# A decoder layer's mixer: the attention halves of the output projection in tiles of their own, the mLSTM output in pairs of heads

## The chip, the cores and the metric

The kernel runs on one core of one Trainium2 chip. The metric is the device time of one execution in microseconds (us). TensorE is the engine for matrix products, VectorE, ScalarE and GpSimd work elementwise, and SyncE issues the transfers from memory.

## The reference, cut to what matters

One layer on 256 tokens of width 1024: a half-step SwiGLU FFN, a mixer, a second half-step FFN, and a last norm. Each of the three parts has its RMS norm, and shift, scale and gate that come from a vector `c` by a matrix `w_ada`. The mixer runs attention (8 heads of 64) beside an mLSTM (4 heads of 128):

```
o_a = rmsnorm(attention(q_a, k_a, v_a), attn_norm)
h_m = (h_m - mu) * rsqrt(var + EPS) * mlstm_norm
o_m = (h_m + mlstm_skip * x_conv) * silu(z)
return concat([o_a, o_m]) @ w_out
```

## The kernel before, in words

All activations lie transposed, 128 features by 256 tokens in a tile; a group of 1024 features is eight tiles. Every big product is made of three products: weight and activation are each split into a rounded high part and a remainder (`whi`, `wlo`; `hh`, `hl`), and `mm3` adds high times high, remainder times high and high times remainder. ScalarE copies the high part, VectorE subtracts for the remainder (`hilo` for activations, `split_piece` for weights, in pieces of 1024 columns).

Weights come in chunks of 1 MB. `weights()` hands out the next chunk; it first asks for the load of the chunk three further on and the split of the next one. There are four buffers of raw chunks and five each of `whi` and `wlo`. The 72 columns of `w_ada` are loads too, 512 KB each into three `ada` buffers, and each is followed by one VectorE product with a sum (`junk`). `side(0)` issues the next such job. All loads go through SyncE's queue in the order in which the program issues them.

The order on the other engines is made by a scheduler, except where `act.on`, `dve.on` or `pe.on` is set: those instructions keep the program's order among themselves. The `junk` products of the mixer keep it too.

The mixer's end, in program order: `tiles(...)` makes the gate `z` in two groups of two heads, each from one chunk, reading all of `hh` and `hl`. Between them stand the last attention heads (`weigh`), the sums of the mLSTM heads (`m_sums`), and `a_out`, which makes the attention's norm, scales the four tiles `oa[j]` in place and splits `oa[0]` into `mix0h` and `mix0l`. After the second gate group come `m_factors` (the mLSTM's norm factors in `rows`, four rows of 256), the split of `oa[1..3]` into `hh[:,1..3]`, the Silu of the gate, and `m_out_pre`. The output projection follows: four chunks of `w_out` of two steps each, k = 0 to 7, each step 24 products. `m_spread` broadcasts `rows` over the partitions into two banks of tag `b`, and `m_out(h)` finishes one head and splits it into `hh[:,4+h]`.

The softmax weights of a pair of attention heads lie in a tile `pr` of 128 x 768 numbers, in two buffers by turns; `turn(j)` transposes them.

Of the kernel before, what the change touches and what calls it, by code (L numbers as in the profile page):

```python
# [11 lines left out]
F32R = mybir.dt.float32r  # L12
BF16 = mybir.dt.bfloat16
AF = mybir.ActivationFunctionType
ALU = mybir.AluOpType
AX = mybir.AxisListType

P = 128
T = 256
# [5 lines left out]
NH = 4  # L25
# [11 lines left out]
C_MN = 124  # L37
C_SK = 128
# [23 lines left out]
def layer(ctx: ExitStack, tc: tile.TileContext, i, out: bass.AP):  # L62
    nc = tc.nc
    act, dve, pool, pe = (Ordered(tc, e) for e in (nc.scalar, nc.vector, nc.gpsimd, nc.tensor))
# [29 lines left out]
    def const(shape, dt, name):  # L94
        return cst.tile(shape, dt, tag=name, name=name)
# [10 lines left out]
    sm = const([P, NSM], F32, "sm")  # L106
# [114 lines left out]
    def weights(ahead=3):  # L221

        n = used[0]
        used[0] += 1
        load_to(n + ahead)
        split_to(n + 1)
        return parts[n]
# [6 lines left out]
    def mm3(ps, w, b0, xh, xl, start, stop):  # L234
        hi, lo = part(w, b0, P)
        pe.matmul(ps, hi, xh, start=start, stop=False, skip_group_check=True)
        pe.matmul(ps, lo, xh, start=False, stop=False, skip_group_check=True)
        pe.matmul(ps, hi, xl, start=False, stop=stop, skip_group_check=True)
# [77 lines left out]
    hh = const([P, ND, WS], F32R, "hh")[:, :, 0:W]  # L316
    hl = const([P, ND, WS], F32R, "hl")[:, :, 0:W]
# [249 lines left out]
    def side(*on):  # L567

        for o in on:
            if jobs:  # L570
                jobs.pop(0)(o)
# [8 lines left out]
    pinned[0] = True  # L580
    for c in range(2):
        w = weights()
        side(*[0] * (2 - c))
        for d4 in range(4):
            d = c * 4 + d4
            for h in range(NH):
                mm3(px[h][:, 0:W], w, d4 * 512 + h * P, hh[:, d], hl[:, d], start=(d == 0), stop=(d == 7))
            if d == 0:
                r = rstd_of([acc, nxt_sq[0]], pre=False)
# [17 lines left out]
def mixer(tc, nc, i, mp, L):  # L607
    act, dve, pool, pe, sp = L["act"], L["dve"], L["pool"], L["pe"], L["sp"]
    nm, bank, t256, as32, dma = L["nm"], L["bank"], L["t256"], L["as32"], L["dma"]
    weights, part, mm3, hilo = L["weights"], L["part"], L["mm3"], L["hilo"]  # L610
    sm, hh, hl, tmp, eps_t = L["sm"], L["hh"], L["hl"], L["tmp"], L["eps_t"]
# [3 lines left out]
    side, jobs = L["side"], L["jobs"]  # L615

    def mt(shape, name, dt=F32, tag=None, bufs=1):
        return mp.tile(shape, dt, name=nm(name), tag=tag or name, bufs=bufs)
# [62 lines left out]
    xc = mt([P, NH, T], "xc")  # L681
# [42 lines left out]
    st = {}  # L724
# [60 lines left out]
    cn = mt([P, NH, T], "cn")  # L785
# [7 lines left out]
    def m_sums(h):  # L793
        if h == 0:
            st["prow"] = bank("a")
        prow = st["prow"]
        pn = bank("b" if h == 3 else "m")
        pe.matmul(pn[:, 0:T], vm[:, 0, h], wE[h][:, 0:T], start=True, stop=False, skip_group_check=True)
        pe.matmul(pn[:, P:T], vm[:, 1, h], wE[h][:, T:384], start=False, stop=True, skip_group_check=True)
        pe.matmul(prow[0:4, 0:T], ohc[:, h], wE[h][:, 0:T], start=(h == 0), stop=False, skip_group_check=True)  # L800
        pe.matmul(prow[0:4, P:T], ohc[:, h], wE[h][:, T:384], start=False, stop=(h == NH - 1),
                  skip_group_check=True)
        act.activation(cn[:, h], pn[:, 0:T], AF.Copy)
        s = st["sq", h] = t256("sq", bufs=3)
        act.activation(s, cn[:, h], AF.Square)

    def m_vars(h):
        pe.matmul(st["prow"][0:4, T:2 * T], ohc[:, h], st["sq", h], start=False, stop=(h == NH - 1),
                  skip_group_check=True)
# [15 lines left out]
        spread(rs)  # L825


    mix0 = [mt([P, T], name, F32R) for name in ("mix0h", "mix0l")]

    def mix(k):  # L830
        return mix0 if k == 0 else (hh[:, k, 0:T], hl[:, k, 0:T])

    zs = mt([P, NH, T], "zs")

    def z_silu(h2):
        z2 = zs[:, 2 * h2:2 * h2 + 2]
        tc.keep_in_program_order(act.activation(z2, z2, AF.Silu))

    def m_out_pre(h):

        dve.scalar_tensor_tensor(cn[:, h], cn[:, h], sm[:, C_MN + h:C_MN + h + 1], zs[:, h], ALU.mult, ALU.mult)
        dve.scalar_tensor_tensor(xc[:, h], xc[:, h], sm[:, C_SK + h:C_SK + h + 1], zs[:, h], ALU.mult, ALU.mult)

    def m_spread():
        st["pb"] = [bank("b") for _ in range(2)]
        for h in range(NH):
            pe.matmul(st["pb"][h // 2][:, h % 2 * T:(h % 2 + 1) * T], ohr[:, h], rows, start=(h % 2 == 0), stop=True,
                      skip_group_check=True)

    def m_out(h):  # L850
        t1 = t256("ht", bufs=3)
        dve.tensor_tensor(t1, cn[:, h], st["pb"][h // 2][:, h % 2 * T:(h % 2 + 1) * T], ALU.mult)
        dve.tensor_tensor(t1, t1, xc[:, h], ALU.add)
        hilo(*mix(4 + h), t1)


    sc = 64 ** -0.5
# [1 line left out]
    oa = mt([P, 4, T + 3], "oa", tag="A")  # L859
# [5 lines left out]
    def scores(j):  # L865
        qa, ka = st["qk", j]
        ps = [bank("a"), bank("a")]
        for e in range(2):
            rw = slice(e * 64, e * 64 + 64)
            pe.matmul(ps[e][:, 0:P], qa[rw, 0:P], ka[rw, 0:P], start=True, stop=False,  # L870
                      skip_group_check=True)
            pe.matmul(ps[e][:, P:384], qa[rw, P:T], ka[rw], start=False, stop=False,
                      skip_group_check=True)
        for e in range(2):
            pe.matmul(ps[e][:, 0:P], ident_b, maskq, start=False, stop=True, skip_group_check=True)
            pe.matmul(ps[e][:, T:384], ident_b, maskq, start=False, stop=True, skip_group_check=True)
        mx = tmp.tile([P, 4], F32, tag="mx", name=nm("mx"), bufs=2)
        for e in range(2):
            dve.tensor_reduce(mx[:, e:e + 1], ps[e][:, 0:P], AX.X, ALU.max, negate=True)
            dve.tensor_reduce(mx[:, 2 + e:3 + e], ps[e][:, P:384], AX.X, ALU.max, negate=True)  # L880
        dve.tensor_scalar(mx, mx, sc, None, ALU.mult)
        pr = st["pr", j] = mt([P, 2, 384], "pr", bufs=2)
        su = tmp.tile([P, 4], F32, tag="su", name=nm("su"), bufs=2)
        ri = tmp.tile([P, 4], F32, tag="ri", name=nm("ri"), bufs=2)
        for e in range(2):
            act.activation(pr[:, e, 0:P], ps[e][:, 0:P], AF.Exp, bias=mx[:, e:e + 1], scale=sc,
                           accum_out=su[:, e:e + 1])
            act.activation(pr[:, e, P:384], ps[e][:, P:384], AF.Exp, bias=mx[:, 2 + e:3 + e], scale=sc,
                           accum_out=su[:, 2 + e:3 + e])
        dve.reciprocal(ri, su)  # L890
        for e in range(2):
            dve.tensor_scalar(pr[:, e, 0:P], pr[:, e, 0:P], ri[:, e:e + 1], None, ALU.mult)
            dve.tensor_scalar(pr[:, e, P:384], pr[:, e, P:384], ri[:, 2 + e:3 + e], None, ALU.mult)
# [36 lines left out]
    def a_out():  # L930
        r2 = rstd_of([acc2, st["osq"]], ones_h, "a", pre=False)
        for j in range(4):
            o = oa[:, j, 0:T]
            dve.scalar_tensor_tensor(o, o, sm[:, C_AN + j:C_AN + j + 1], r2, ALU.mult, ALU.mult)
            if j == 0:
                hilo(*mix(0), o)


    side(1, 0)
# [40 lines left out]
    next(g0)  # L980
    weigh(1)
    scores(3)
    m_sums(0)
    next(g0)
    turn(2)
    m_scores(3)
    m_sums(1)
    g = tiles(shifted(zs[:, 0]), shifted(zs[:, 1]))
    side(0, 0, 0, 0, 0)
    next(g)  # L990
    next(g0)
    turn(3)
# [7 lines left out]
    next(g)  # L1000
    act.on = dve.on = False
    m_sums(3)
    m_vars(1)
    m_vars(2)
    g = tiles(shifted(zs[:, 2]), shifted(zs[:, 3]))
    side(0, 0, 0, 0)
    next(g)
    m_vars(3)
    m_factors()
    next(g)  # L1010
    for j in range(1, 4):
        hilo(*mix(j), oa[:, j, 0:T])
    z_silu(0)
    z_silu(1)
    for h in range(NH):
        m_out_pre(h)
    act.on = dve.on = False
    po = [bank(t) for t in ("m", "m", "a", "a")]
    for c in range(4):
        w = weights()  # L1020
        side(*[0] * c if c > 1 else ())
        pe.on = c < 2
        for k2 in range(2):
            k = c * 2 + k2
            for d in range(8):
                mm3(po[d // 2][:, (d % 2) * T:(d % 2 + 1) * T], w, (k2 * 8 + d) * P, *mix(k),
                    start=(c == 0 and k2 == 0 and d % 2 == 0), stop=(c == 3 and k2 == 1))
                if (k, d) == (2, 7):
                    m_spread()
                    for h in range(NH):  # L1030
                        m_out(h)
    side(*[0] * len(jobs))
    act.on = dve.on = True
    L["pre_shift"](2)
# [89 lines left out]
```

## Time and profile before

| | us |
|---|---|
| runs of the kernel: median (lowest to highest of 3) | 536.26 (535.54 to 536.56) |
| the profiled execution | 536.01 |
| its span, first to last instruction | 534.2 |
| TensorE busy | 513.6 (96%) |
| VectorE busy | 425.7 (80%) |
| ScalarE busy | 281.9 (53%) |
| mean granted TensorE clock | 0.988 |

The profiled execution took 1.8 us more than its span; what starts and ends it lies outside the span. The span has three parts: the first FFN to about 195 us, the mixer to about 333 us, and the second FFN with the last norm.

### The profile page before, as it was taken

The page shows a single profiled execution, that of the slowest core. Times are in us where ns is not written, and L with a number is a line of the kernel's source. Part 1 is how long each engine was busy: PE and PEld are TensorE (multiplying, and loading weights), DVE is VectorE, ACT ScalarE, POOL GpSimd, SP SyncE. Part 2 cuts the span into 40 slices and gives each one's busy share as a digit, 9 for nine tenths or more (in the row PEclk, how much of TensorE's full clock was granted, in tenths as well). Part 3 has the DMA queues.
Part 4 walks back from the last instruction along what each step waited for, and adds up shares of the span by engine and source line. Part 5 has one row for each costly group of instructions (what it writes and reads, how often), then busy time and mean ns, then how long its engine had stood idle before and what let it go on. Part 6 is the DMA issues. An engine that isn't in the chain of part 4 may idle for free.

```text
span 534.2 us, 9598 instructions
## 1 busy us (share of the span) xinstructions
PE 513.6 (96%) x3826; PEld 481.8 (90%) x3826; DVE 425.7 (80%) x717; ACT 281.9 (53%) x484; POOL 46.9 (9%) x60
## 2 busy tenths in 40 slices
PE   8999999999999999999998889999999999999992
PEld 7889999999988889988877689999999999988892
DVE  7799978988889897988867978979986776655433
ACT  4364446665544554569665454866555455544410
POOL 5000000000011210220100000400000000022320
PEclk9999999999999999999999979999999999999997
DMA  8999985677778886882117564377865455455002
GB/s 312 351 362 383 388 341 217 250 264 298 307 295 320 343 337 251 307 310 102 41 40 276 241 252 158 146 309 276 318 237 195 158 195 199 159 205 190 1 1 79
DMA packets 24095, 125.73 MB, mean 235 GB/s; under 512 B 2673, under 2 KB 3185, under 8 KB 14578
## 3 DMA queue, kind: packets, MB, share of 16 engines
q1 hardware_dynamic: 23762, 124.72, 62.0%
q8 instruction: 30, 0.49, 0.4%
q10 hardware_dynamic: 288, 0.39, 0.2%
q14 instruction: 15, 0.12, 0.1%
HBM read 124.05 MB, written 1.05 MB: 234 GB/s over the span
## 4 chain that ended last, share of the span: by engine, by line
PE 88%; DVE 4%; DMA 4%; ACT 2%; issue 1%; SPq 0%; DVEq 0%; ACTq 0%
PE psa L55 44%; PE psb L55 24%; PE psm L55 20%; DMA raw<-in_gu 2%; DMA ada<-in_ada 1%; DMA raw<-in_wout 1%; ACT whi L55 1%; DVE wlo L55 1%; DVE junk L55 1%; DVE x L55 1%; DVE ht L55 0%; SPq L98 0%; DVE u_out L55 0%; DVE nw L55 0%; DVE oa L55 0%
## 5 line engine op out<-in xcount | busy, mean ns | idle before, releaser
L55 ACT ACTIVATE whi<-raw 128x1024 fp32r<-128x1024 f32 (+1 forms) x160 | 166.9, 1047 | 125.1 <-PE psa L55 78.7
L55 DVE TENSOR_TENSOR wlo<-raw,whi 128x1024 fp32r<-128x1024 f32 (+1 forms) x160 | 193.0, 1210 | 44.1 <-ACT whi L55 42.7
L55 PE MATMUL psa<-hh,wlo 128*128 128x256 f32 (+1 forms) x452 | 127.1, 282 | 0.0
L55 PE MATMUL psa<-hh,whi 128*128 128x256 f32 (+1 forms) x452 | 126.8, 282 | 0.2 <-DVE x L55 0.2
L55 PE MATMUL psa<-hl,whi 128*128 128x256 f32 (+1 forms) x452 | 125.0, 281 | 0.0
L55 DVE SCALAR_TENSOR_TENSOR junk<-ada,c_bc 128x1024 bf16<-128x1024 f32 x72 | 89.4, 1241 | 10.0 <-DMA ada<-in_ada 9.4
L55 PEld LDWEIGHTS psa<-hh,whi 128*128 128x128 f32 x452 | 85.5, 189 | 0.4 <-DVE x L55 0.4
L55 PEld LDWEIGHTS psa<-hh,wlo 128*128 128x128 f32 x452 | 85.6, 189 | 0.1
L55 PEld LDWEIGHTS psa<-hl,whi 128*128 128x128 f32 x452 | 84.9, 189 | 0.1
L55 PE MATMUL psb<-hh,whi 128*128 128x258 f32 (+1 forms) x284 | 82.0, 289 | 0.6 <-ACT whi L55 0.6
L55 PE MATMUL psb<-hh,wlo 128*128 128x258 f32 (+1 forms) x284 | 80.4, 284 | 0.4 <-DVE wlo L55 0.4
L55 PE MATMUL psb<-hl,whi 128*128 128x258 f32 (+1 forms) x284 | 79.8, 283 | 0.3 <-DVE hl L55 0.3
L55 PE MATMUL psa<-g,whi 128*128 128x512 f32 (+1 forms) x198 | 59.9, 370 | 0.0
L55 PEld LDWEIGHTS psb<-hh,whi 128*128 128x128 f32 x284 | 53.7, 189 | 2.6 <-ACT whi L55 1.0
L55 PEld LDWEIGHTS psb<-hh,wlo 128*128 128x128 f32 x284 | 53.8, 190 | 1.8 <-issue 1.0
L55 PEld LDWEIGHTS psb<-hl,whi 128*128 128x128 f32 x284 | 53.6, 190 | 0.5 <-DVE hl L55 0.5
L55 PE MATMUL psm<-hh,whi 128*128 128x256 f32 (+1 forms) x168 | 47.8, 286 | 4.7 <-ACT hh L55 4.7
L55 PE MATMUL psm<-hl,whi 128*128 128x256 f32 (+1 forms) x168 | 47.2, 285 | 0.7 <-DVE hl L55 0.7
L55 PE MATMUL psm<-hh,wlo 128*128 128x256 f32 (+1 forms) x168 | 47.6, 284 | 0.0
L55 PE MATMUL psa<-g,wlo 128*128 128x256 f32 x176 | 46.0, 281 | 0.0
L55 PEld LDWEIGHTS psa<-g,whi 128*128 128x128 f32 x198 | 35.3, 188 | 6.3
L55 PEld LDWEIGHTS psm<-hh,whi 128*128 128x128 f32 x168 | 32.2, 192 | 5.1 <-ACT hh L55 4.9
(238 smaller groups left out, 756.6 us busy)
## 6 DMA issues: line engine op xcount, KB each, us to landing
ada<-in_ada SPq DMA_DIRECT2D x72, 512.0 KB, 5.7
raw<-in_dn SPq DMA_DIRECT2D x22, 1024.0 KB, 4.8
raw<-in_guB SPq DMA_DIRECT2D x19, 1024.0 KB, 4.8
raw<-in_gu SPq DMA_DIRECT2D x18, 1024.0 KB, 7.1
raw<-in_gu SPq DMA_DIRECT2D x8, 512.0 KB, 7.4
raw<-in_wqk SPq DMA_DIRECT2D x4, 1024.0 KB, 5.8
raw<-in_wout SPq DMA_DIRECT2D x4, 1024.0 KB, 5.4
raw<-in_guA SPq DMA_DIRECT2D x4, 768.0 KB, 8.3
```

The source lines that it names most:

```text
L55: r = f(*a, **k)
```

## The change

- The split of `oa[1..3]` goes into two new tiles, `mix3h` and `mix3l`, of 128 x 3 x 256 numbers, which take the place of the softmax weights (tag `pr`). It is one `hilo` of 768 columns, in `a_out`, behind the split of `oa[0]`.
- `m_spread` stands behind k = 1 instead of k = 2. `m_out` works on two heads at once, in program order on ScalarE and VectorE, with three operations and a split of 512 columns, and `m_out_pre` is gone.
- ScalarE puts `mlstm_norm` on `cn` as it copies it out of the bank, and `mlstm_skip` on `xc` (`m_skip`, four copies in place). The square for the variance reads the bank.
- The ada jobs are dealt out anew: the projections' three all stand at the first chunk; in the mixer one goes behind `scores(3)`, six (five before) to the first gate group, one (four before) to the second, and one to the second chunk of `w_out`.

```diff
-        side(*[0] * (2 - c))
+        side(*[0] * (3 - 3 * c))
...
-        act.activation(cn[:, h], pn[:, 0:T], AF.Copy)
+        act.activation(cn[:, h], pn[:, 0:T], AF.Copy, scale=sm[:, C_MN + h:C_MN + h + 1])
         s = st["sq", h] = t256("sq", bufs=3)
-        act.activation(s, cn[:, h], AF.Square)
+        act.activation(s, pn[:, 0:T], AF.Square)
...
-    mix0 = [mt([P, T], name, F32R) for name in ("mix0h", "mix0l")]
+    mix0, mix3 = [mt([P, T], name, F32R) for name in ("mix0h", "mix0l")], []
...
-        return mix0 if k == 0 else (hh[:, k, 0:T], hl[:, k, 0:T])
+        return mix0 if k == 0 else [t[:, k - 1] for t in mix3] if k < 4 else (hh[:, k, 0:T], hl[:, k, 0:T])
...
-    def m_out_pre(h):
-
-        dve.scalar_tensor_tensor(cn[:, h], cn[:, h], sm[:, C_MN + h:C_MN + h + 1], zs[:, h], ALU.mult, ALU.mult)
-        dve.scalar_tensor_tensor(xc[:, h], xc[:, h], sm[:, C_SK + h:C_SK + h + 1], zs[:, h], ALU.mult, ALU.mult)
...
-    def m_out(h):
-        t1 = t256("ht", bufs=3)
-        dve.tensor_tensor(t1, cn[:, h], st["pb"][h // 2][:, h % 2 * T:(h % 2 + 1) * T], ALU.mult)
-        dve.tensor_tensor(t1, t1, xc[:, h], ALU.add)
-        hilo(*mix(4 + h), t1)
+    def m_skip():
+        for h in range(NH):
+            act.activation(xc[:, h], xc[:, h], AF.Copy, scale=sm[:, C_SK + h:C_SK + h + 1])
+
+    def m_out(h2):
+
+        h = slice(2 * h2, 2 * h2 + 2)
+        c = cn[:, h]
+        dve.tensor_tensor(c, c, st["pb"][h2].rearrange("p (h t) -> p h t", t=T), ALU.mult)
+        dve.tensor_tensor(c, c, xc[:, h], ALU.add)
+        dve.tensor_tensor(c, c, zs[:, h], ALU.mult)
+        k = slice(4 + 2 * h2, 6 + 2 * h2)
+        hilo(hh[:, k, 0:T], hl[:, k, 0:T], c)
...
             dve.scalar_tensor_tensor(o, o, sm[:, C_AN + j:C_AN + j + 1], r2, ALU.mult, ALU.mult)
-            if j == 0:
-                hilo(*mix(0), o)
+
+        mix3[:] = [mt([P, 3, T], name, F32R, tag="pr", bufs=2) for name in ("mix3h", "mix3l")]
+        hilo(*mix0, oa[:, 0, 0:T])
+        hilo(*mix3, oa[:, 1:4, 0:T])
...
     scores(3)
+    side(0)
     m_sums(0)
...
-    side(0, 0, 0, 0, 0)
+    side(0, 0, 0, 0, 0, 0)
...
     m_sums(3)
+    m_skip()
...
-    side(0, 0, 0, 0)
+    side(0)
...
-    for j in range(1, 4):
-        hilo(*mix(j), oa[:, j, 0:T])
     z_silu(0)
     z_silu(1)
-    for h in range(NH):
-        m_out_pre(h)
...
-        side(*[0] * c if c > 1 else ())
+        side(*[0] * (0, 1, 2, 3)[c])
...
-                if (k, d) == (2, 7):
+                if (k, d) == (1, 7):
                     m_spread()
-                    for h in range(NH):
-                        m_out(h)
+                    act.on = dve.on = True
+                    m_out(0)
+                    m_out(1)
+                    act.on = dve.on = False
```

## Rows read from the trace of the kernel before

**Rows 1.** TensorE's waits, 196 to 345 us: total, times, longest

```profile
PE psm L55 <- ACT hh L55: 4.7, 1, 4.7
PE psa L55 <- ACT va L55: 1.4, 1, 1.4
PE psm L55 <- DVE hl L55: 0.7, 1, 0.7
```

**Rows 2.** TensorE's timeline around k = 0, k = 1 and the broadcast: start, duration

```profile
301.59 0.28 PE L55 MATMUL psm<-mix0h,whi 128*128 128x256 f32 x1
...
304.34 0.28 PE L55 MATMUL psa<-mix0l,whi 128*128 128x256 f32 x1
309.35 0.58 PE L55 MATMUL psm<-hh,whi 128*128 128x256 f32 x1 [4.73 <-ACT hh L55]
...
314.08 0.28 PE L55 MATMUL psm<-hh,whi 128*128 128x256 f32 x1
...
317.02 0.73 PE L55 MATMUL psb<-rows,ohr 36*128 36x256 f32 x4
```

**Rows 3.** Stretches: length, busy of each engine, granted clock, DMA share, GB/s

```profile
200.00:230.00 30.00, 30.00 (x244) 29.44 (x244) 25.77 (x50) 15.89 (x29) 4.26 (x5) 1.00 0.77 283
295.00:332.80 37.80, 32.39 (x247) 31.14 (x247) 32.42 (x67) 17.20 (x32) 0.00 (x0) 0.91 0.59 226
304.60:309.30 4.70, 0.02 (x1) 0.00 (x0) 3.75 (x6) 2.68 (x7) 0.00 (x0) 0.70 1.00 417
309.30:314.10 4.80, 4.75 (x25) 4.75 (x26) 3.31 (x9) 3.04 (x5) 0.00 (x0) 0.58 1.02 416
```

**Rows 4.** ScalarE's timeline ahead of k = 1

```profile
292.85 1.06 ACT L55 ACTIVATE whi<-raw 128x1024 fp32r<-128x1024 f32 x1 [1.95 <-PE psb L55]
...
304.10 2.00 ACT L55 ACTIVATE whi<-raw 128x1024 fp32r<-128x1024 f32 x2 [0.30 <-DMA raw<-in_wout]
...
308.48 0.51 ACT L55 ACTIVATE zs<-ht,col 128x256 f32<-128x256 f32 x1 [2.02 <-DVE ht L55]
308.90 1.01 ACT L55 ACTIVATE hh<-oa 128x256 fp32r<-128x256 f32 x3
309.93 1.28 ACT L55 ACT_TABLE_LOAD   x1
```

**Rows 5.** VectorE's timeline, 277 to 309 us

```profile
277.71 0.18 DVE L55 RECIPROCAL ri<-su 128x4 f32<-128x4 f32 x1 [2.70 <-ACT pr L55]
...
290.93 0.43 DVE L55 SCALAR_TENSOR_TENSOR nw<-rr 128x256 f32<-128x256 f32 x1 [1.86 <-ACT rr L55]
...
302.83 1.20 DVE L55 SCALAR_TENSOR_TENSOR junk<-ada,c_bc 128x1024 bf16<-128x1024 f32 x1
...
305.20 2.35 DVE L55 TENSOR_TENSOR wlo<-raw,whi 128x1024 fp32r<-128x1024 f32 x2
307.58 0.42 DVE L55 TENSOR_TENSOR rows<-rs,rows 4x256 fp32r<-4x256 f32 x1
308.02 0.42 DVE L55 TENSOR_TENSOR ht<-rr,psb 128x256 f32<-128x256 f32 x1
```

**Rows 6.** SyncE's queue: the issues around two w_out chunks

```profile
283.73 0.38 SPq L98 DMA_DIRECT2D raw<-in_wout  x1
...
298.19 0.33 SPq L98 DMA_DIRECT2D ada<-in_ada  x1
298.57 0.90 SPq L98 DMA_DIRECT2D raw<-in_wout  x2
```

**Rows 7.** Groups by shape: count, busy us, mean ns of one

```profile
L55 DVE SCALAR_TENSOR_TENSOR cn<-cn,sm,zs 128x256 f32<-128x256 f32 x4 | 1.9, 479 | 1.5 <-ACT zs L55 1.5
...
L55 ACT ACTIVATE hh<-x,gs 128x256 fp32r<-128x256 f32 x16 | 7.6, 495 | 1.2 <-DVE x L55 1.2
...
L55 DVE TENSOR_TENSOR half<-half,psa 128x512 f32<-128x512 f32 x8 | 5.5, 682 | 0.5 <-PE psa L55 0.4
...
L55 ACT ACTIVATE zs<-zs 128x512 f32<-128x512 f32 x2 | 1.1, 621 | 0.0
```

## Prediction

> **What bounds the kernel now.** I read the page first: TensorE is busy 96% of the span, so only its gaps can be won back. The list of TensorE's waits over the mixer (196 to 345 us) comes next. It holds one large wait, 4.7 us for ScalarE's `hh` tile, and small ones: 1.4 us for `va` and 0.7 us for `hl` [rows 1]. TensorE's own timeline shows where the large one lies: the 24 products of the first w_out step (k = 0) run from 301.59 us to the last at 304.34, and the first product of k = 1 starts at 309.35, 4.73 us idle [rows 2]. The table of stretches adds that the granted clock falls to 0.70 in the gap and to 0.58 after it, that is, the lower of the two levels for most of that stretch [rows 3]. The reader should see that at that clock k = 1 takes from 309.35 to 314.08, 4.73 us, where k = 0 took 304.34 + 0.12 - 301.59 = 2.87.
>
> The timelines of the other engines say why `hh` is late. ScalarE splits `oa[1..3]` into `hh` at 308.90, behind the gate's `zs` at 308.48, because both are held in program order [rows 4]. That `zs` waited 2.02 us for VectorE's `ht` at 308.02, which sits behind `rows` at 307.58 and two weight splits of 2.35 us from 305.20 [rows 5]. Those splits wait for ScalarE's halves at 304.10, and these for a w_out chunk that SyncE issued only at 298.57, after the ada load at 298.19 [rows 4, 6]. But the root is a place in memory: k = 1 reads `hh[:,1]`, and `hh` holds the gate projection's input until its last product, just before 301.59. In `hh` the split can't be made earlier, wherever it stands in the program.
>
> **Part 1: the split of `oa[1..3]` gets the softmax weights' tiles.** `mix3h` and `mix3l` rotate into the two `pr` buffers, whose last reader is the transpose in `turn(3)`, ahead of `a_out` in TensorE's order. So the splits can run in `a_out`. Its refinement starts at 290.93 [rows 5] and takes 3 x 0.42 + 4 x 0.48 = 3.2 us with the four scalings, so the splits come at 294 to 296 us, and k = 1 no longer waits for anything from the gate. The price is one ScalarE copy of 768 columns, between 0.62 us (512 columns) and 1.00 (half of the two splits of 1024) [rows 4, 7], and one VectorE subtraction between 0.68 (512) and 1.18 (half of 2.35) [rows 5, 7], in place of three small ones each of about 0.34 to 0.42. They stand before the second gate group's `ht`, where TensorE has other products to do. Gain: 4.73 us of wait, and 4.73 - 2.87 = 1.86 us of slow clock, 6.59 together.
>
> **Part 2: the broadcast moves from behind k = 2 to behind k = 1.** `m_spread` is four products, 0.73 us before and after [rows 2]. In the new order TensorE comes to it at 304.46 + 2.87 = 307.33. It needs `rows` (end 307.58 + 0.42 = 308.00 now) and a bank that the last `ht` frees (308.02 + 0.42 = 308.44 now) [rows 5]. If VectorE's order stays as it is, TensorE waits 308.44 - 307.33 = 1.11 us there, with k = 2 queued behind. But two of VectorE's four ada products that now stand in the chain before `rows` (the last at 302.83, 1.20 us) leave it; of the four at the second gate group one remains. If `rows` and `ht` come 1.1 us or more earlier, the wait is nothing. Bounds 0 and 1.11; I take 0.5, the middle, since the weight splits between them can land on either side.
>
> **Part 3: the mLSTM output in pairs.** Removed from VectorE: eight scalings (0.48 us each [rows 7]) and twelve operations of 256 columns (0.42 [rows 5]), 8 x 0.48 + 12 x 0.42 = 8.9 us. Added: eight of 512 columns at 0.68 [rows 7], 5.5 us. ScalarE gets four more scaled copies at about 0.50, like `hh<-x,gs` [rows 7], for the skip path; the norm's scale rides on the `cn` copy that exists, worth at most 0.1 each. k = 4 needs the first pair at 307.33 + 0.5 + 0.73 + 2 x 2.87 = 314.3. The pair's first multiply follows the broadcast at 308.5; its third waits for the Silu. The gate's `zs` ends at 308.99 at the latest, the table load takes 1.28 and the Silu 0.62 [rows 4, 7], so 310.9; then 0.68 + 0.62 + 0.68 for multiply, ScalarE's half and the remainder: 312.9. That is 1.4 us of margin, so this part costs nothing, and it takes away the present wait of 0.7 for `hl` at k = 4 [rows 1]: gain 0.68. With no cover, if another weight split (1.18) and its ScalarE half (1.00) stand in front, it costs 1.18 + 1.00 - 1.4 = 0.8.
>
> The Trainium skill (ScalarE: Activation LUTs, "What ACT_TABLE_LOAD costs") adds a drain of about 1.38 us to every switch of table. The trace shows a load of 1.28 us and the Silu directly behind it, so I leave the drain out; by the page the pair would come at 314.3, the whole margin would be gone, and the sum would stay.
>
> ScalarE is busy 17.20 us of the 37.80 from 295 to 332.8, VectorE 32.42 [rows 3]; a scaled copy at 0.50 on the one costs as much as the 0.48 on the other, so the move is hidden by ScalarE's free time. If the four copies stood ahead of the factor chain, `rows` would come 4 x 0.50 = 2.0 us later; that is the bound. The Trainium skill (ScalarE: Activation LUTs, "Rules for kernel authors") says to put multiplications on VectorE, not ScalarE. These rows don't bear that out for fp32; by the rule the sum would lose up to those 2.0 us.
>
> **Part 4: the ada jobs.** Three jobs leave the stretch before the second gate group: one goes behind `scores(3)`, one to the first gate group, one to k = 2. The chunk issued at 298.57 then waits for eight ada loads, not nine, and I expect it before 292 us. The chunk at 283.73 [rows 6] waits for seven, not five; each load waits for the product three before it. VectorE takes on two more products ahead of the attention norm, 2 x 1.20 = 2.4 us. It has 2.70 us idle until 277.71 and 1.86 until 290.93 [rows 5], which cover them if one falls into the first hole. If not, the first 2.70 stays unused, 2.4 - 1.86 = 0.5 us reaches the norm, or one product (1.20) stands ahead of the values that TensorE waits for (`va`, 1.4 now [rows 1]). Also `cn`'s bank is held for the square as well, some 0.4 longer. Bounds 0 and 1.6; I take 0.4, as the holes fit. The third job of the projections moves one chunk ahead; TensorE is busy 30.00 of 30.00 us there [rows 3], which hides it; without that it is one product's 1.2.
>
> **The sum.** 4.73 + 1.86 + 0.68 = 7.27 won; 0.5 + 0.4 lost: 6.4 net. The profiled execution took 536.01 us (span 534.2 and 1.8 around it), so 529.6; the median is 0.25 above it, so 529.9. After the mixer TensorE runs through, so what is won stays won. VectorE keeps up: from 295 us on it has about 32.4 - 2 x 1.2 - 3.4 = 26.6 us of work in 37.8 - 7.3 = 30.5, 87%, and 32.4 of 37.8 is 86% now.
>
> **The rivals.**
> *A: half of it comes back.* The broadcast waits the full 1.11, the pairs 0.8, the `va` side 1.6: 7.27 - 3.5 = 3.8 us net, 532.5; with `rows` 2.0 later behind the skip copies, 1.8 net, 534.5. For it: VectorE is 86% busy and its order is made anew. Against: each of these has a cover.
> *B: slower, by the w_out chunk behind seven ada loads.* If VectorE takes its extra products late, the seventh load is issued at about 290 and the chunk after it. A chunk takes 5.4 us to land (298.57 to the release at about 304.0 [rows 4, 6]), so 296 or later. ScalarE's split of that chunk, now at 292.85 [rows 4], would hold its in-order queue, with `cn`, the norm and the gate's `zs` behind it, and TensorE before the second gate group. It decides from 6.4 us of hold, a chunk landing after 299; at 301 the kernel takes 538. For it: SyncE's queue is in order and already waits for products. Against: that needs the load to wait 7 us more than the one product moved ahead explains.
> *C: the change doesn't do what it says.* The split in `mix3` is placed late all the same, because the order is pinned behind the norm, or the wait is replaced by `rows` in full. Then k = 1 or the broadcast waits 4 to 5 us: within 0.2%, 536.
>
> **How the numbers follow.** Chances: forecast (528.4 to 531.3) 0.62, A (531.3 to 535.2) 0.20, C 0.07, B 0.11. Within 0.2% means within 1.1 us, about what a measurement tells from no change here. Faster is forecast and A, 0.82; same 0.07; slower 0.11. The range goes from 528.4 (net 7.8: all terms at their best, and a short `va` wait gone) to 535.0; it leaves out B, C and a little of A.
>
> **What would show it.** After: no wait of TensorE for `hh` between k = 0 and k = 1; granted clock 1.00 through w_out; `mix3h` before 296 us; the broadcast right after k = 1, with a wait under 1.2 us; no wait for `hl` at k = 4; the w_out chunk issued before 292; ffn2's first products some 6 us earlier. It is wrong if a wait of over 3 us stands before the broadcast, at the second gate group or at the values.

## The result, and the profile after

The changed kernel takes 533.3 us (median of 20 runs, 531.46 to 536.59) against 536.39 for the kernel before (20 runs); the ratio is 0.9944, with 95% interval 0.9934 to 0.9955. So it is about 3.0 us faster, where I forecast 6.4. The profiled execution took 531.47 us, span 529.7, mean granted clock 0.995; it is among the fastest of the 20.

TensorE's waits over the mixer, 190 to 345 us, in the kernel after (total, times, longest; compare [rows 1]):

```profile
PE psm L55 <- ACT hh L55: 1.7, 1, 1.7
PE psb L55 <- DVE rows L55: 1.2, 1, 1.2
PE psa L55 <- ACT va L55: 0.6, 1, 0.6
PE psm L55 <- DVE hl L55: 0.4, 1, 0.4
PE psb L55 <- DVE ht L55: 0.2, 1, 0.2
```

The wait of 4.73 us ahead of k = 1 is gone, but the list hasn't become empty: the waits for `rows`, for `hh` at k = 6 and for `ht` are new, and of the one for `hl` at k = 4 (0.68 before) 0.37 is left. TensorE's timeline after (compare [rows 2]) says where:

```profile
298.25 0.39 PE L55 MATMUL psb<-hh,whi 128*128 128x258 f32 x1 [0.18 <-DVE ht L55]
...
301.23 0.28 PE L55 MATMUL psm<-mix0h,whi 128*128 128x256 f32 x1
...
304.10 0.29 PE L55 MATMUL psm<-mix3h,whi 128*128 128x256 f32 x1
...
308.36 0.92 PE L55 MATMUL psb<-rows,ohr 36*128 36x256 f32 x4 [1.24 <-DVE rows L55]
...
316.48 0.39 PE L55 MATMUL psm<-hl,whi 128*128 128x256 f32 x1 [0.37 <-DVE hl L55]
...
323.15 0.39 PE L55 MATMUL psm<-hh,whi 128*128 128x256 f32 x1 [1.67 <-ACT hh L55]
```

k = 1 follows k = 0 with no gap, and k = 0 to k = 1 is the computed 2.87 us. The broadcast waits 1.24, k = 4 waits 0.37 for the first pair's remainder and k = 6 waits 1.67 for the second pair's half. From k = 0 to ffn2's first product are 28.03 us (301.23 to 329.26), where before had 31.23 (301.59 to 332.82) and my sum 31.23 - 7.27 + 0.5 = 24.5.

VectorE's timeline after (compare [rows 5]) shows its order, and this was the reading that mattered most:

```profile
290.32 0.43 DVE L55 SCALAR_TENSOR_TENSOR nw<-rr 128x256 f32<-128x256 f32 x1
291.79 1.22 DVE L55 SCALAR_TENSOR_TENSOR junk<-ada,c_bc 128x1024 bf16<-128x1024 f32 x1 [1.04 <-DMA ada<-in_ada]
...
301.25 0.41 DVE L55 SCALAR_TENSOR_TENSOR vv<-psa,dd 4x256 f32<-4x256 f32 x1
302.52 1.23 DVE L55 TENSOR_TENSOR wlo<-raw,whi 128x1024 fp32r<-128x1024 f32 x1 [0.86 <-ACT whi L55]
303.67 0.41 DVE L55 SCALAR_TENSOR_TENSOR nw<-rs 4x256 f32<-4x256 f32 x1
...
305.40 1.23 DVE L55 TENSOR_TENSOR wlo<-raw,whi 128x1024 fp32r<-128x1024 f32 x1 [0.43 <-ACT whi L55]
306.54 1.22 DVE L55 SCALAR_TENSOR_TENSOR junk<-ada,c_bc 128x1024 bf16<-128x1024 f32 x1
...
307.79 0.41 DVE L55 TENSOR_TENSOR rows<-rs,rows 4x256 fp32r<-4x256 f32 x1
...
320.42 1.22 DVE L55 SCALAR_TENSOR_TENSOR junk<-ada,c_bc 128x1024 bf16<-128x1024 f32 x1
...
321.57 0.69 DVE L55 TENSOR_TENSOR cn<-cn,zs 128x512 f32<-128x512 f32 x1
```

The `junk` lines are ada products. One stands inside the refinement of the attention norm and waits there 1.04 us for its load; the next, the new job of the second w_out chunk, stands at 306.54 directly ahead of `rows`; one at 314.59 stands ahead of the first pair's remainder, and two more (316.94 and 320.42) delay the second pair. ScalarE's timeline after (compare [rows 4]) adds the last link:

```profile
294.34 1.06 ACT L55 ACTIVATE whi<-raw 128x1024 fp32r<-128x1024 f32 x1 [0.69 <-DMA raw<-in_wout]
...
295.61 0.83 ACT L55 ACTIVATE mix3h<-oa 128x768 fp32r<-128x768 f32 x1
...
301.43 1.06 ACT L55 ACTIVATE whi<-raw 128x1024 fp32r<-128x1024 f32 x1 [0.95 <-PE psb L55]
302.40 0.40 ACT L55 ACTIVATE rs<-vv 4x256 f32<-4x256 f32 x1
...
304.30 1.06 ACT L55 ACTIVATE whi<-raw 128x1024 fp32r<-128x1024 f32 x1 [1.06 <-PE psa L55]
305.27 0.40 ACT L55 ACTIVATE rows<-rs 4x256 fp32r<-4x256 f32 x1
...
309.23 1.28 ACT L55 ACT_TABLE_LOAD   x1
310.52 1.16 ACT L55 ACTIVATE zs<-zs 128x512 f32<-128x512 f32 x2
...
321.53 1.06 ACT L55 ACTIVATE whi<-raw 128x1024 fp32r<-128x1024 f32 x1 [2.20 <-PE psa L55]
322.49 0.61 ACT L55 ACTIVATE hh<-cn 128x512 fp32r<-128x512 f32 x1
```

The weight split at 304.30 waits for TensorE to release a buffer, which it does with k = 0's last product. From there it is a fixed run: 1.06 for ScalarE's half, 1.23 for VectorE's remainder at 305.40, 1.22 for the ada product, 0.41 for `rows`, ended at 308.20. TensorE has only k = 1's 2.87 us to fill it.

### The profile page after: what moved, and what is told of

The parts are those of the page before. It is cut to its first block, busy times and chain, and to the rows that moved or that the text cites. A ratio compares the mean times of both kernels' runs of the same rounds, so it can differ in the third digit from the quotient of the medians.

```text
span 529.7 us, 9595 instructions
## 1 busy us (share of the span) xinstructions
PE 511.9 (97%) x3826; PEld 480.0 (91%) x3826; DVE 422.3 (80%) x703; ACT 282.9 (53%) x484; POOL 45.5 (9%) x60
## 4 chain that ended last, share of the span: by engine, by line
PE 87%; DVE 6%; DMA 3%; ACT 2%; issue 1%; SPq 0%; DVEq 0%; ACTq 0%
PE psa L55 44%; PE psb L55 24%; PE psm L55 19%; DVE junk L55 2%; DMA ada<-in_ada 2%; DVE wlo L55 1%; ACT whi L55 1%; DMA x<-in_x 1%; DVE u_out L55 0%; DVE ht L55 0%; ACT sq L55 0%; DVE oa L55 0%; DVE hl L55 0%; DVE nw L55 0%; ACT hh L55 0%
## 5 line engine op out<-in xcount | busy, mean ns | idle before, releaser
L55 PE MATMUL psa<-hh,wlo 128*128 128x256 f32 (+1 forms) x440 | 123.3, 281 | 0.0
L55 PE MATMUL psa<-hh,whi 128*128 128x256 f32 (+1 forms) x440 | 123.1, 282 | 0.0
L55 PE MATMUL psa<-hl,whi 128*128 128x256 f32 (+1 forms) x440 | 122.1, 280 | 0.0
L55 PEld LDWEIGHTS psa<-hh,wlo 128*128 128x128 f32 x440 | 83.1, 189 | 0.1
L55 PEld LDWEIGHTS psa<-hh,whi 128*128 128x128 f32 x440 | 82.9, 189 | 0.0
L55 PEld LDWEIGHTS psa<-hl,whi 128*128 128x128 f32 x440 | 82.7, 189 | 0.0
L55 PE MATMUL psm<-hh,whi 128*128 128x256 f32 (+1 forms) x156 | 43.9, 282 | 1.7 <-ACT hh L55 1.7
L55 PE MATMUL psm<-hl,whi 128*128 128x256 f32 (+1 forms) x156 | 43.7, 282 | 0.5 <-DVE hl L55 0.4
L55 PE MATMUL psm<-hh,wlo 128*128 128x256 f32 (+1 forms) x156 | 43.8, 281 | 0.0
L55 PEld LDWEIGHTS psa<-g,wlo 128*128 128x128 f32 x176 | 32.1, 188 | 0.6
```

Source lines behind the costliest of these rows:

```text
L55: r = f(*a, **k)
```

## The experiments

Theory 1 says that the new places of the ada jobs eat the gain; 1a to 1c split it by place (jobs put later, jobs put earlier, jobs taken out of the factor chain, that is, of the steps that make `rows`: `dd` and `vv` on VectorE, the logarithm and the exponential `rs` on ScalarE, the Newton steps `nw` and `rs` on VectorE, and the copies into `rows`). By Theory 2 the loss lies in the other parts of the change. The experiments changed one part each; ratios are to the kernel before on the same chip (medians 535.92 to 536.51).

**The tiles alone**, in the kernel before.

```diff
...
-            if j == 0:
-                hilo(*mix(0), o)
+
+        mix3[:] = [mt([P, 3, T], name, F32R, tag="pr", bufs=2) for name in ("mix3h", "mix3l")]
+        hilo(*mix0, oa[:, 0, 0:T])
+        hilo(*mix3, oa[:, 1:4, 0:T])
...
-    for j in range(1, 4):
-        hilo(*mix(j), oa[:, j, 0:T])
```

> The kernel before with only the new tiles for the split of oa[1..3]; jobs, broadcast and mLSTM output as before. Theory 1 (the tiles bring the gain; about 3.3 us are lost again to VectorE's order around the output projection, where ada products and weight splits stand ahead of rows and inside the pairs): no wait of TensorE between k = 0 and k = 1, the broadcast behind k = 2 waits for nothing, hl waits under 1.5 us; 530 to 533 us. Theory 2 (the gain needs the pairs and the earlier broadcast too): waits at k = 4 grow to 3 us or more, and the time is 534 or more.

534.45 us, ratio 0.9964 [0.9952, 0.9976]. TensorE's waits in its trace:

```profile
PE psm L55 <- ACT hh L55: 2.8, 1, 2.8
PE psm L55 <- DVE hl L55: 1.6, 1, 1.6
PE psa L55 <- ACT va L55: 1.4, 1, 1.4
```

The wait at k = 1 is gone, but a new one of 2.84 stands at 316.70 for `hh` of the first mLSTM head, then 1.62 for its `hl`, and the granted clock is 0.50 from 320 to 324 us. The time is that of Theory 2, and the two waits at k = 4 come to 4.5 us. The 6.59 that I credited to the tiles brings 1.9 (0.0036 of 536) without the other parts: TensorE comes to k = 4 6.7 us earlier (313.86 against 320.53), but its `hh` only 2.8 us (316.23 against 319.00).

**The ada jobs where the kernel before has them**, the rest as changed.

```diff
-        side(*[0] * (3 - 3 * c))
+        side(*[0] * (2 - c))
...
     scores(3)
-    side(0)
...
-    side(0, 0, 0, 0, 0, 0)
+    side(0, 0, 0, 0, 0)
...
-    side(0)
+    side(0, 0, 0, 0)
...
-        side(*[0] * (0, 1, 2, 3)[c])
+        side(*[0] * c if c > 1 else ())
```

> The changed kernel with the ada jobs where the kernel before has them. Theory 1: no ada product stands ahead of rows behind the second gate group's own four, but the four delay rows by about as much, so a wait of 0.5 to 1.5 us stays at the broadcast; the waits inside the pairs shrink; 531 to 533.5 us. Theory 2 (the pairs themselves are late, wherever the jobs stand): the waits for hl and hh at k = 4 and k = 6 stay at 2 us together; time as the changed kernel, 533.3.

527.64 us (527.11 to 527.87), ratio 0.9836 [0.9824, 0.9849]: the fastest version of all, 8.8 us below before, and faster than either theory had it. Its waits, and VectorE's order in the factor chain:

```profile
PE psb L55 <- DVE rows L55: 0.7, 1, 0.7
PE psa L55 <- ACT va L55: 0.6, 1, 0.6
```

```profile
300.08 1.21 DVE L55 SCALAR_TENSOR_TENSOR junk<-ada,c_bc 128x1024 bf16<-128x1024 f32 x1
...
301.22 0.41 DVE L55 SCALAR_TENSOR_TENSOR vv<-psa,dd 4x256 f32<-4x256 f32 x1
301.56 1.20 DVE L55 SCALAR_TENSOR_TENSOR junk<-ada,c_bc 128x1024 bf16<-128x1024 f32 x1
...
302.70 0.41 DVE L55 SCALAR_TENSOR_TENSOR nw<-rs 4x256 f32<-4x256 f32 x1
...
303.93 2.34 DVE L55 TENSOR_TENSOR wlo<-raw,whi 128x1024 fp32r<-128x1024 f32 x2
306.30 0.41 DVE L55 TENSOR_TENSOR rows<-rs,rows 4x256 fp32r<-4x256 f32 x1
```

The two products cost the chain nothing here. With them its first Newton step (`nw`) starts 2.38 us after k = 0 does (302.70 against 300.32); after, with both taken away, 2.44 (303.67 against 301.23). There `vv` does start earlier, 0.02 us after k = 0 instead of 0.90, but ScalarE has a weight split at 301.43 ahead of the logarithm, and VectorE its remainder at 302.52 ahead of the Newton step. `rows` comes 5.98 us after k = 0 starts; after, 6.56. The clock is 1.00 through w_out, and k = 0 to ffn2 takes 24.56 us.

**Four ada products left out**, the changed kernel otherwise.

```diff
...
+        if 52 <= col < 56:
+            return
         t = wp.tile([P, D], F32, tag="ada", name=nm("ada"), bufs=3)
```

> The changed kernel with the last four ada jobs of the mixer left out (their loads and VectorE products; four columns of the last norm's shift are zero instead). Theory 1: the waits for rows (1.24) and for hh at k = 6 (1.67) go, and with them what the slower executions lose; 528 to 530.5 us, and the executions lie within 1.5 us of each other. Theory 2: the wait for hh at k = 6 stays over 1 us, 531 or more. If the spread of the executions (531.5 to 536.6) comes from elsewhere than these waits, it stays.

529.0 us (527.42 to 531.06), ratio 0.9867 [0.9846, 0.9887]. Without the products that fall late, the waits for `rows`, `hl` and `hh` are gone. What is left is 1.61 us for the second gate group's `ht`, since a product inside the norm's refinement waits 2.47 us for its load. The kernel wins back 3.5 of the 5.2 us between the changed kernel and the fastest version (0.9933 - 0.9867 of 0.9933 - 0.9836), but this doesn't price the moved job alone: it does less work, and three of the four products stand at the output projection in the fastest version too, where no wait follows. The spread of the runs, 3.6 us, didn't shrink as expected, so the waits for `rows`, `hl` and `hh` aren't all of its cause.

**The changed kernel again**, on the chip of the three runs above.

> The changed kernel as it is, once more, for a second trace and for its spread. Both theories: 533.3 us median, executions 531.4 to 536.6. If the slower executions lose to a lower granted clock behind the short waits, a trace of one of over 533 shows a stretch under 1.00 behind rows or hh; if they lose to transfers, it shows longer waits at full clock.

532.38 us (531.25 to 534.86), ratio 0.9933 [0.9912, 0.9954]. The waits for `rows`, `hl` and `hh` are 1.24, 0.37 and 1.67 once more; `ht` is 1.27 instead of 0.18. The stretches behind the broadcast (length, busy of each engine, granted clock, DMA share, GB/s) differ from those of the first profile, where the clock was 1.00:

```profile
310.00:312.00 2.00, 2.00 (x12) 1.86 (x13) 1.97 (x3) 1.97 (x3) 0.00 (x0) 0.78 0.71 282
312.00:314.00 2.00, 2.00 (x12) 2.00 (x11) 0.94 (x2) 0.80 (x2) 0.00 (x0) 0.50 0.60 229
314.00:316.00 2.00, 2.00 (x17) 2.00 (x17) 0.00 (x0) 1.00 (x2) 0.00 (x0) 0.87 0.01 2
```

An estimate from these rows of what the lower level costs this execution is 2 x 0.22 + 2 x 0.50 + 2 x 0.13 = 1.7 us.

**The new job places alone**, in the kernel before: the edit of the second experiment, reversed.

> The kernel before with only the new places of the ada jobs. If the new places cost by themselves, by the two early products in the norm and the one ahead of rows, then hh's wait at k = 1 moves with ht and rows: 537 to 539 us. If they only hurt where the tiles have already taken the wait of k = 1 away, the gap at k = 1 hides them: 536 to 537. If fewer products in the factor chain let the gate finish earlier, as I had reckoned, 533.5 to 535.5.

537.69 us (536.18 to 540.88), ratio 1.0034 [1.0017, 1.0051], slower by some 1.8, as the first of the three expectations had it. The wait ahead of k = 1 is 5.29 us instead of 4.73. So Part 4 is a loss under both kernels, larger (5.2 to 5.8 us) where the old wait no longer covers it.

**One job late, two jobs early**: the fastest version, with one job of the second gate group moved to the second w_out chunk; and with two of them moved ahead, one behind `scores(3)` and one to the first gate group.

```diff
-    side(0, 0, 0, 0)
+    side(0, 0, 0)
...
-        side(*[0] * c if c > 1 else ())
+        side(*[0] * (0, 1, 2, 3)[c])
```

> As e2 (changed kernel, jobs as before), but one of the four jobs of the second gate group moved to the second w_out chunk, as the change does. Theory 1a (that product lands ahead of rows, where it holds the broadcast): TensorE waits 1.3 to 2 us for rows instead of 0.66; 528 to 529.5 us. Theory 1b (the loss of the changed kernel is from the two products moved ahead of the attention norm): no change against e2, 527.6.

```diff
     scores(3)
+    side(0)
...
-    side(0, 0, 0, 0, 0)
+    side(0, 0, 0, 0, 0, 0)
...
-    side(0, 0, 0, 0)
+    side(0, 0)
```

> As e2, but two of the four jobs of the second gate group moved ahead of the attention norm, one behind scores(3) and one to the first gate group, as the change does. Theory 1b: the last of them waits 1 to 2.5 us for its load inside the norm's refinement, TensorE waits 0.2 to 1.7 us for ht before the second gate group, the executions spread over 2 us or more; 528.5 to 531. Theory 1a: no change against e2, 527.6, spread under 1 us.

531.42 us, 0.9924 [0.9911, 0.9938], and 533.0 us, 0.9945 [0.9933, 0.9958]. Both are slower than either theory had them: 1a had a wait of at most 2 us in the first and no change in the second, 1b no change in the first and at most 531 in the second. A single moved job costs 4.7 us (0.9924 - 0.9836, times 536). Both have the same wait for `rows`, 2.94 us. In the first the granted clock behind it is 0.50 from 310 to 316 us, which costs some 3.4 (6 x 0.50, and 0.4 for 0.80 in the 2 us behind); 2.94 - 0.66 + 3.4 = 5.7 is close to the 5.8 between the two spans (531.1 and 525.3). In the second no job came late at all, and `rows` is late all the same: what they share is that products left the factor chain.

**Five jobs, and three, at the second gate group**, the remaining one and three at the third w_out chunk: this takes the product ahead of `rows` away and asks only what happens in the chain.

```diff
-    side(0, 0, 0, 0)
+    side(0, 0, 0, 0, 0)
...
-        side(*[0] * c if c > 1 else ())
+        side(*[0] * (0, 0, 1, 3)[c])
```

> As e2, but with five jobs instead of four at the second gate group and one instead of two at the third w_out chunk. If a product is free where VectorE waits for ScalarE in the factor chain, the wait for rows grows by the fifth product, which now stands between two steps of the refinement, by up to 1.2 us: 528 to 529. If a product between the pairs cost more, 527.0 to 527.5.

```diff
-    side(0, 0, 0, 0)
+    side(0, 0, 0)
...
-        side(*[0] * c if c > 1 else ())
+        side(*[0] * (0, 0, 3, 3)[c])
```

> As e2, but one of the four jobs of the second gate group goes to the third w_out chunk, behind the pairs in the program. No ada product then stands ahead of rows. Theory 1a in its first form (an ada product ahead of rows is what holds the broadcast): the wait for rows is under 0.7 us, 527 to 527.8. Theory 1c (what matters is that the product leaves the factor chain: a weight split slips into its place, and then a third split, whose buffer TensorE frees only at the end of k = 1, stands ahead of rows): the wait is 2.5 to 3 us as in e5, with a low clock behind it, 531 to 532.5.

531.54 us, 0.9913 [0.9901, 0.9926], and 532.36 us, 0.9919 [0.9906, 0.9932]. The expectation for five was missed: TensorE waits 2.92 for `rows`, as two weight splits at 306.88 stand in front, whose halves came late because ScalarE waited 2.55 us for a w_out chunk. With three, the wait and the time are those of 1c, and not of 1a in its first form; VectorE's timeline shows it plainest:

```profile
302.01 1.23 DVE L55 TENSOR_TENSOR wlo<-raw,whi 128x1024 fp32r<-128x1024 f32 x1
...
304.88 1.23 DVE L55 TENSOR_TENSOR wlo<-raw,whi 128x1024 fp32r<-128x1024 f32 x1 [0.88 <-ACT whi L55]
...
307.73 1.23 DVE L55 TENSOR_TENSOR wlo<-raw,whi 128x1024 fp32r<-128x1024 f32 x1 [1.30 <-ACT whi L55]
308.98 0.42 DVE L55 TENSOR_TENSOR rows<-rs,rows 4x256 fp32r<-4x256 f32 x1
```

ScalarE's half of that last split, on its timeline:

```profile
306.64 1.06 ACT L55 ACTIVATE whi<-raw 128x1024 fp32r<-128x1024 f32 x1 [1.79 <-PE psa L55]
307.60 0.40 ACT L55 ACTIVATE rows<-rs 4x256 fp32r<-4x256 f32 x1
```

No ada product stands between the Newton steps and `rows`, and yet TensorE waits 2.94 for it. A weight split has slipped into the hole at 302.01, so all later splits stand one place further ahead; the third now needs a buffer that TensorE frees only at the end of k = 1, and `rows` is queued behind it on VectorE and on ScalarE. TensorE waits for `rows` right there, so it waits for its own release: 1.06 + 1.23 + 0.42 us and the gaps between. That would explain why the wait is 2.94 in three kernels to the hundredth, and 1.24 in both profiles of the changed one: the loop starts at TensorE's own last product, and as long as it stands nothing done earlier shortens it. The figure alone doesn't tell, though: the 2.92 with five jobs comes from a load. And the chain in front is late too. Without the third split `rows` could follow the last Newton step, which ends at 306.43 here and at 308.03 in the version with two jobs early; with the 1.04 us from there to the broadcast in the next trace below, an estimate of the wait that would be left is 0.9 and 1.8 us. The 1.67 at k = 6 is of the kind, too, but only by a little: the split at 321.53 waits for k = 5's end, and `hh` stands behind it, 1.06 + 0.61; VectorE's last product for `hh`, late behind the ada product at 320.42, ends at 322.26, 0.23 us before `hh` starts.

**A sixth buffer for ScalarE's halves**, in the kernel with three jobs, as the direct test of the loop (the place comes from a smaller tile of zeros).

```diff
...
-        hi = wp.tile([P, SP], F32R, tag="whi", name=nm("whi"), bufs=5)
+        hi = wp.tile([P, SP], F32R, tag="whi", name=nm("whi"), bufs=6)
```

> The kernel with three jobs in the second gate group and three at the third w_out chunk, with six buffers instead of five for ScalarE's halves of the split weights (VectorE's remainders keep five); the place comes from a tile of zeros of half the size. Theory 1c (the 2.94 us wait for rows is a loop: a weight split ahead of rows waits for the buffer that TensorE frees with k = 1's last product): the loop is broken or shortened by ScalarE's 1.06 us at least, so the wait before the broadcast is between 0.5 and 1.9 us, the granted clock behind it mostly 1.00, and the time 528 to 530.5 us. Rival (rows is late through its own chain of sums, logarithm and Newton steps without the products, whatever the buffers): the wait stays between 2.5 and 3.0 us and the time at 531.5 to 532.5.

532.55 us (531.25 to 532.79), ratio 0.9931 [0.9917, 0.9944]. The wait is 2.96: 1c missed its numbers, and those of its rival came, to 0.05 us of the time. VectorE's timeline shows what stands in front of `rows`:

```profile
306.32 1.23 DVE L55 TENSOR_TENSOR wlo<-raw,whi 128x1024 fp32r<-128x1024 f32 x1 [0.47 <-PE psa L55]
307.46 0.40 DVE L55 SCALAR_TENSOR_TENSOR nw<-vv,nw 4x256 f32<-4x256 f32 x1
307.90 0.41 DVE L55 SCALAR_TENSOR_TENSOR rs<-nw,rs 4x256 f32<-4x256 f32 x1
308.79 0.41 DVE L55 TENSOR_TENSOR rows<-rs,rows 4x256 fp32r<-4x256 f32 x1 [0.48 <-ACT rows L55]
```

Now it is VectorE's own half of the split, still with five buffers, that waits for TensorE's end of k = 1 (306.25), and the scheduler has put it further ahead, into the Newton steps: 1.23, then two steps, ScalarE's `rows` (0.41) and VectorE's (0.41). What ScalarE's half no longer adds, these add. So a release by TensorE stands ahead of `rows` once more, where the rival had only the chain; but one buffer doesn't open the loop, and no run has. That the loop sets the wait is read from the traces, and not shown by a run in which it is gone.

**The broadcast behind k = 2 again**, in the fastest version.

```diff
-                if (k, d) == (1, 7):
+                if (k, d) == (2, 7):
```

> As e2, with the broadcast behind k = 2, where the kernel before has it. If its earlier place is worth something, the pairs come later and TensorE waits 1 to 3 us for hl at k = 4: 528.5 to 530.5. If not, the wait for rows (0.66) goes and the time is 527.0.

529.74 us, 0.9897 [0.9879, 0.9915], a time as expected: 3.3 us of the gain are the earlier broadcast's. Behind k = 2 the broadcast doesn't wait, but the second pair comes late, 1.67 for `hh` at 320.62 and then 0.83 for `hl`.

**Four ada buffers instead of three**, in the changed kernel (paid for by a smaller tile of zeros).

```diff
...
-        t = wp.tile([P, D], F32, tag="ada", name=nm("ada"), bufs=3)
+        t = wp.tile([P, D], F32, tag="ada", name=nm("ada"), bufs=4)
```

> The changed kernel with four ada buffers in place of three (a tile of zeros at the start is halved to make room), VectorE's order around the norm unchanged. Theory 1b with the load as its cause: the loads are issued one product earlier, no product waits for its load inside the refinement, no wait for ht stays, no low clock behind the waits; 530.5 to 531.3 us, spread under 1.5 us. If the spread has another cause, it stays at 3 us or more.

533.37 us, 0.9947 [0.9934, 0.9961]; the expectation was missed. No product waits for its load any more, and the times spread over 0.9 us only, but nothing is won: ScalarE waits 2.15 us for a w_out chunk at 292.75, `ht` 0.54, and `rows` (1.24), `hl` (0.36) and `hh` (1.67) are where they were.

## Why the predicted time was too low

- **Part 1** was right in its mechanism: `mix3h` starts at 295.61 (before 296 was forecast) and takes 0.83, `mix3l` 0.95, both inside their bounds, and k = 1 waits for nothing. But the 6.59 belongs to parts 1 to 3 together. The ladder (ratios times 536 us): tiles alone -1.9; with the pairs, the skip copies and the norm's scale, broadcast behind k = 2, -5.5; with the earlier broadcast -8.8; with the new job places -3.0 (-3.6 in the second comparison).
- **Part 2**, sized 0.5 between 0 and 1.11: 0.66 in the fastest version, 1.24 with the new places. The argument that `rows` comes earlier when ada products leave its chain was false: three of the four left it, not two, and `rows` came later (6.56 us after k = 0 against 5.98).
- **Part 3**: the sizes held (0.68 to 0.69 for an operation of 512 columns; 0.53 for a skip copy against 0.50). In the fastest version the pairs cost nothing, as forecast, and the 0.68 at k = 4 is gone. In the changed kernel they wait 0.37 and 1.67, since ada products and splits stand between their operations. The row for the table load is again 1.28 us, with the Silu beginning 0.01 behind it. The Trainium skill (ScalarE: Activation LUTs, "What ACT_TABLE_LOAD costs") adds a drain of about 1.38 us; this trace doesn't show it.
- **Part 4 is the step that failed.** I priced the new job places at 0.4, "as the holes fit", and the job put to the second w_out chunk at nothing, as I took it to run behind `m_out`. Measured, Part 4 costs 5.2 to 5.8 us (0.9933 or 0.9944 against 0.9836). I looked for holes into which the moved products could go, and not at what the scheduler puts in the places that they leave, nor at where the job of the second chunk would land (306.54, directly ahead of `rows`). The w_out chunk of 298.57 is issued at 289.49, before 292 as forecast, but what it was to bring was misread: the two splits at 305.20 [rows 5] show no wait, so VectorE's operations ahead of them, and not the chunk, set their time.
- **Without that part the sum was nearly right, and too low:** 7.27 - 0.5 = 6.8 forecast, 8.8 measured. Two terms were missing from the sum: 0.76 at the values, whose wait of 1.36 falls to 0.60 (the range had it, the sum not), and 0.95 in the second FFN, from its first product to the end (201.4 and 200.4 us), of which waits of 0.16 and 0.25 at its start are a part and the rest wasn't followed.
- **The rivals:** A had the time (532.5) and two of its three places, but not the cause, so that its time came near is luck. B shows in small, as holds of ScalarE by a w_out chunk of 0.69 and 2.15 us; the chunk at 283.73 [rows 6] is issued at 287.59. C didn't happen.

**Open:** the 1.24 us wait for `rows` is followed by the lower clock level in two profiled executions (0.50 from 312 to 314 us in the changed kernel again and with four ada buffers) and by 1.00 in the first, with the same waits for `rows` and `hh` and, to 0.01 us, for `hl`. The wait for `ht` some 10 us ahead differed (1.27, 0.54 and 0.18), but no run changed that alone, so this isn't settled. Nor was the loop opened: a sixth buffer for both halves of the split weights, or an order with `rows` held ahead of the splits, wasn't tried. And how the loss of Part 4 divides among the single jobs isn't known: one job late costs 4.7 us and two early 5.8, where all of them together cost 5.2 to 5.8.

## What to carry to other kernels

A small operation between the steps of a chain that runs over several engines can be free where it is, as the two ada products were; before moving it, ask what the scheduler will put into the hole, and which buffer that newcomer waits for. A wait that comes out the same to the hundredth in execution after execution may be a loop that starts at the waiting engine's own release: look for the split or load ahead of the needed operation before you look for more speed upstream. And time the parts of a change one by one: here one part of four took back well over half of what the other three had won.

## What the runs showed of the hardware

I hadn't expected waits this short to be followed by the lower clock level: TensorE's 1.24 us of idle time was followed by 0.50 in two executions and by 1.00 in one, the 2.94 us by 0.50 over 6 us (310 to 316) with one job late and with two jobs early, and by 0.67 and 0.50 over 4 us in the one with three jobs in the chain. A wait of 1.61 us for `ht`, in the run with four products left out, was followed by 1.00. The 0.66 us wait of the fastest version was followed by 1.00, and its four runs lie within 0.8 us of each other, where the six of the changed kernel spread over 3.6 on the same chip.
